# Ten gates projected inside a merge stage: all in the first two branches, or spread over four

## The chip, the cores and the metric

One core of a Trainium2 chip runs the whole program, one decoder layer on 1024 tokens of width 1024. The time is device microseconds of one execution, as the median of several runs; smaller is better. Engines are named as the profile names them: PE is the matmul engine (PEld its weight loads), DVE the vector engine, ACT the scalar engine, POOL GpSimd, and SP the engine whose queue issues every DMA of this kernel.

## The reference, cut to what matters

The mixer projects the normalised input h to the inputs of four token mixers and to four gates of 1024 channels. The outputs of the mixers are projected, multiplied by the sigmoid of their gate, summed, and projected once more.

```python
z = h @ w_in
(u_a, q_b, k_b, v_b, q_c, k_c, v_c, q_d, k_d, v_d, qi_d, ki_d, wi_d, gates) = jnp.split(z, SPLIT_POINTS, axis=-1)
o_a = conformer_conv(...); o_b = diff_attention(...)
o_c = stick_breaking_attention(...); o_d = dsa_attention(...)
g = sigmoid(gates).reshape(b, s_len, 4, 1024)
merged = g[:, :, 0] * (o_a @ w_branch[0])
for i, o in ((1, o_b), (2, o_c), (3, o_d)):
    merged = merged + g[:, :, i] * (o @ w_branch[i])
return merged @ w_out
```

A gated FFN follows, which the change doesn't touch.

## The kernel before

All tiles are held transposed, 128 channels on the partitions and 1024 tokens along the free axis. There are 4 x 8 = 32 gate tiles; (br, c) is channel block c of branch br. Matmuls work on two float32r parts, high and low: split_w (L178) loads a raw weight tile of 512 KB into one of two wr buffers, casts the high part on ACT and subtracts the low part on POOL, or on the engine handed in. A gate projection, proj (L356), takes 2 halves x 8 k x 3 products, 48 matmuls, and reads the input hH and hL; its weights lie in the four wp buffers, a pair for each gate. Its results go through two PSUM buffers (pmm).

The first 22 gates in the order of the list gq (L540) are projected ahead of the merge by gate_tile (L542), which stores the raw result in the scratch sg_s; PE does that between the steps of the attention branches. Ten are left in gq when the merge begins.

The merge (L902) goes through the branches in the order 3, 2, 1, 0. For each it splits two k halves of the branch's output (from o_s) and of its weights (L905, L908, low parts on DVE), eight tiles of the twelve in pool obp; then for each c it gets the gate in a buffer sg, one of three in pool sgp. Where the gate is still in gq it is projected there and ACT writes its sigmoid out of PSUM (L914): a live gate. Otherwise SP loads it from the scratch and ACT applies the sigmoid in place (L917). A branch tile of 12 matmuls (L925) goes into one of two PSUM buffers (pss); DVE multiplies it by sg (L928), and for all but the first branch the product is added to accs[c] (L930), on POOL for branches 2 and 1, on DVE for branch 0. As gq keeps (2,6), (2,7) and (3,0) to (3,7), all live gates lie in the first two branches of the merge.

Behind it the sum is split into mhi (ACT, L947) and mlo (DVE, L948), in two halves of 512 tokens, and the output projection (L968) runs over row tiles t. Half 0 lies in pool big, which is opened where hH and hL end; half 1 in pool mg, which is opened where sgp ends.

The order of instructions on each engine is fixed at build time by a planner: it goes by program order, but puts what it holds to be ready ahead of what it holds to be waiting; buffers of one pool go round in program order. On the chip each engine takes its instructions in that order and waits where one isn't ready.

Of the kernel before, what the change touches and what calls it, by code (L numbers as in the profile page):

```python
# [25 lines left out]
NK = D // P  # L26
# [86 lines left out]
def tile_hybrid_block(ctx, tc, x, pos, ada, pk, cst, w_in, w_br, w_out, w_up, w_dn, out):  # L113
    nc = tc.nc

    def pool(name, bufs, space=None, side=None):
        kw = {} if space is None else {"space": space}
        return tc.tile_pool(name=name, bufs=bufs, side=side, reuse_waits="tile", **kw)
# [3 lines left out]
    def dma(o, i):  # L122
        return nc.sync.dma_start(o, i)  # L123
# [54 lines left out]
    def split_w(src, wpool=None, E=None):  # L178
        wpool = wpool or wp
        raw = wr.tile([P, D], F32, name="wraw", tag="w")  # L180
        dma(raw, src)
        hi = wpool.tile([P, D], F32R, name="whi", tag="w")
        lo = wpool.tile([P, D], F32R, name="wlo", tag="w")
        A.copy(hi, raw)  # L184
        (E or G).tensor_tensor(out=lo, in0=raw, in1=hi.bitcast(F32), op=OP.subtract)  # L185
        return hi, lo
# [72 lines left out]
    pmm = psx.enter_context(pool("pmm", 2, PSUM))  # L259
    ptt = psx.enter_context(pool("ptt", 2, PSUM))  # L260

    NSPILL = 22
    HP = 100000
    hi_pri = ExitStack()
    mrg = ExitStack()
# [3 lines left out]
    with ExitStack() as mix:  # L269
# [86 lines left out]
        def proj(name, i, consume):  # L356
            hi, lo = split_w(w_in[W_INDEX[(name, i)]])
            for hf in range(2):
                ps = pmm.tile([P, 512], F32, name="mm", tag="mm")
                n = 0  # L360
                cs = slice(hf * 512, hf * 512 + 512)
                for k in range(NK):
                    ks = slice(k * P, (k + 1) * P)
                    for a, b in ((hi, hH), (hi, hL), (lo, hH)):
                        PE.matmul(ps, a[:, ks], b[:, k, cs], start=(n == 0), stop=(n == 3 * NK - 1))  # L365
                        n += 1
                consume(hf, cs, ps)
# [121 lines left out]
        with pool("scp", 1) as scp, ExitStack() as scx:  # L489
# [47 lines left out]
                proj(name, i, consume)  # L537
                store_hl(name, i, hi, lo, 2, 64, False)

            gq = [(br, c) for br in range(4) for c in range(NK)]  # L540

            def gate_tile():  # L542
                br, c = gq.pop(0)

                def consume(hf, cs, ps):
                    o = gtp.tile([P, 512], F32, name="gt", tag="g")
                    A.copy(o, ps)
                    dma(sg_s[br * NK + c][:, cs], o)
                proj("g", br * NK + c, consume)
# [35 lines left out]
            with pool("rad", 1) as rad, pool("radj", 1) as radj, pool("rada", 1) as rada:  # L585
# [58 lines left out]
                for t in A_T + V_T:  # L644
                    c = off[t - 2]
# [4 lines left out]
                for t in A_T + V_T:  # L650
# [5 lines left out]
                    c = off[t - 2]  # L656
# [196 lines left out]
                dma(o_s[2 + pr], oT)  # L853

        hi_pri.close()
        while len(gq) > 32 - NSPILL:
            gate_tile()

        hcs = []
# [41 lines left out]
        with pool("sgp", 3, side="right") as sgp:  # L901
            for bi, br in enumerate((3, 2, 1, 0)):  # L902
                oh, ol, wh, wl = [], [], [], []
                for k in range(2):
                    hi, lo = split_w(o_s[2 * br + k], obp, V)  # L905
                    oh.append(hi)
                    ol.append(lo)
                    a, b = split_w(w_br[2 * br + k], obp, V)  # L908
                    wh.append(a)
                    wl.append(b)  # L910
                for c in range(NK):
                    sg = sgp.tile([P, S], F32, name="sgl", tag="w")
                    if (br, c) in gq:
                        proj("g", br * NK + c, lambda hf, cs, ps: A.activation(sg[:, cs], ps, AF.Sigmoid))  # L914
                    else:
                        dma(sg, sg_s[br * NK + c])
                        A.activation(sg, sg, AF.Sigmoid)  # L917
                    ccs = slice(c * P, (c + 1) * P)
                    ps = pss.tile([P, S], F32, name="brp", tag="s")
                    for hf in range(2):  # L920
                        cs = slice(hf * 512, hf * 512 + 512)
                        n = 0
                        for k in range(2):
                            for a, b in ((wh, oh), (wh, ol), (wl, oh)):
                                PE.matmul(ps[:, cs], a[k][:, ccs], b[k][:, cs], start=(n == 0), stop=(n == 5))  # L925
                                n += 1
                    dst = accs[c] if bi == 0 else sg
                    V.tensor_tensor(out=dst, in0=ps, in1=sg, op=OP.mult)  # L928
                    if bi:
                        (G if br else V).tensor_tensor(out=accs[c], in0=accs[c], in1=sg, op=OP.add)  # L930
# [199 lines left out]
def build(nc, arrays):  # L1130
    import concourse.tile as _tile
    args = {n: nc.dram_tensor("in_" + n, a.shape, mybir.dt.from_np(a.dtype), kind="ExternalInput").ap()
            for n, a in arrays.items()}
    o = nc.dram_tensor("out_y", (S, D), F32, kind="ExternalOutput").ap()
    with _tile.TileContext(nc) as tc:  # L1135
        r = tile_hybrid_block(tc, *args.values(), o)
    return r
# [10 lines left out]
```

## Time and profile before

| | us |
|---|---|
| three runs, median | 2032.14 |
| lowest and highest | 2029.38, 2036.47 |
| profiled execution | 2032.69 |
| its span, first to last instruction | 2030.9 |
| PE busy | 1855.4 (91% of the span) |
| DVE busy | 1154.4 (57%) |
| ACT busy | 829.5 (41%) |
| POOL busy | 472.9 (23%) |

The rows below come from one profiled execution. Times of a row are microseconds from the start of the span. A row of the timeline gives start, duration, engine, line, operation, what it writes and reads, its count where several are merged, and in brackets how long the engine had stood idle before it and what ended that. PE rows overlap, as matmuls are pipelined: the distance of two starts, not the duration, is what one costs. A row of the table by stretches gives, for each engine, its busy time and instructions, then the granted clock of PE (1.00 is full speed), the share of DMA time and the GB/s.

### The profile page before, as it was taken

Reading aid. Unit: us, or ns where it says so; the run is one execution under the profiler, and the core shown is the slowest. Engines: PE = TensorE matmul, PEld = TensorE weight load, DVE = VectorE, ACT = ScalarE, POOL = GpSimd, SP = SyncE. Lnnn points to the kernel's source line nnn. Section 1 sums busy time; section 2 is a strip of 40 time slices with the busy share of each in tenths; the row PEclk is TensorE's granted clock in tenths of the full one; section 3 lists DMA queues with packets and bytes.
Section 4 is the critical chain, followed back from the end, with each engine's and each line's share of the span. In section 5 each row is a group of like instructions: output and inputs, shape, how many; then the busy total and the mean of one; then the engine's idle time right before and its main releaser. Section 6 shows DMA issues by size and latency. Waiting matters only on the chain. (4 is left out here: it accounts for less than half of the span.)

```text
span 2030.9 us, 22858 instructions
## 1 busy us (share of the span) xinstructions
PE 1855.4 (91%) x8792; PEld 1443.3 (71%) x8792; DVE 1154.4 (57%) x1731; ACT 829.5 (41%) x1458; POOL 472.9 (23%) x244
## 2 busy tenths in 40 slices
PE   6888877499999999899999899999999999999996
PEld 3655555376767776677787668788888888888875
DVE  6759999605899857685113765532343334433457
ACT  5556666236545645463222444333122212221122
POOL 0102145272111110011205610222122212222024
PEclk9988989699999999899999999999999999999999
DMA  8364423444514242513113632121111101111114
GB/s 312 94 165 151 174 84 93 126 92 104 187 57 125 78 129 69 147 42 115 62 63 129 225 122 83 63 73 42 32 63 58 47 32 52 62 52 42 32 62 145
DMA packets 61038, 197.30 MB, mean 97 GB/s; under 512 B 9153, under 2 KB 9281, under 8 KB 60929
## 3 DMA queue, kind: packets, MB, share of 16 engines
q1 hardware_dynamic: 60928, 195.84, 30.6%
q8 instruction: 69, 1.13, 0.2%
q14 instruction: 41, 0.33, 0.1%
HBM read 154.13 MB, written 41.68 MB: 96 GB/s over the span
## 5 line engine op out<-in xcount | busy, mean ns | idle before, releaser
L185 POOL TENSOR_TENSOR wlo<-wraw,whi 128x1024 fp32r<-128x1024 f32 x126 | 317.4, 2521 | 1384.2 <-ACT whi L184 1348.2
L365 PE MATMUL mm<-hH,whi 128*128 128x512 f32 x864 | 353.5, 409 | 49.6 <-ACT whi L184 31.5
L365 PE MATMUL mm<-hH,wlo 128*128 128x512 f32 x864 | 350.4, 406 | 3.7 <-POOL wlo L185 3.7
L365 PE MATMUL mm<-hL,whi 128*128 128x512 f32 x864 | 351.9, 407 | 0.9 <-DVE hL L321 0.9
L184 ACT CAST whi<-wraw 128x1024 fp32r<-128x1024 f32 x144 | 150.6, 1049 | 413.2 <-PE ups L1017 283.7
L1017 PE MATMUL ups<-h2h,whi 128*128 128x512 f32 x704 | 277.6, 395 | 1.3 <-DVE h2h L994 1.3
L1017 PE MATMUL ups<-h2l,whi 128*128 128x512 f32 x704 | 277.5, 394 | 0.5 <-DVE h2l L995 0.5
L1017 PE MATMUL ups<-h2h,wlo 128*128 128x512 f32 x704 | 274.5, 390 | 0.0
L1022 DVE SCALAR_TENSOR_TENSOR u<-ups,pkt,u 128x1023 f32<-128x1023 f32 x44 | 56.4, 1283 | 350.8 <-ACT u L1021 350.8
L365 PEld LDWEIGHTS mm<-hH,whi 128*128 128x128 f32 x864 | 166.6, 193 | 95.6 <-ACT whi L184 32.0
L365 PEld LDWEIGHTS mm<-hH,wlo 128*128 128x128 f32 x864 | 166.5, 193 | 41.4 <-POOL wlo L185 4.8
L365 PEld LDWEIGHTS mm<-hL,whi 128*128 128x128 f32 x864 | 167.2, 194 | 36.1 <-issue 2.6
L1017 PEld LDWEIGHTS ups<-h2h,whi 128*128 128x128 f32 x704 | 132.6, 188 | 32.3 <-DVE h2h L994 1.7
L1017 PEld LDWEIGHTS ups<-h2h,wlo 128*128 128x128 f32 x704 | 132.5, 188 | 29.8
L1017 PEld LDWEIGHTS ups<-h2l,whi 128*128 128x128 f32 x704 | 132.7, 189 | 28.2 <-DVE h2l L995 1.0
L1052 DVE TENSOR_TENSOR ya<-ya,dps 128x1024 f32<-128x1024 f32 x80 | 97.3, 1217 | 58.8 <-PE dps L1047 58.6
L605 DVE TENSOR_SCALAR_CACHE_REDUCE junkb<-key,cf 128x1024 bf16<-128x1024 uint16 (+3 forms) x124 | 117.3, 946 | 4.3
L1047 PE MATMUL dps<-whi,ah 128*128 128x512 f32 x352 | 109.4, 392 | 5.5 <-DVE ya L1052 5.5
L1047 PE MATMUL dps<-wlo,ah 128*128 128x512 f32 x352 | 108.6, 390 | 0.0
L1047 PE MATMUL dps<-whi,al 128*128 128x512 f32 x352 | 108.4, 389 | 0.0
L872 DVE SCALAR_TENSOR_TENSOR hc<-hpad,pkt,hc 128x1024 f32<-128x1024 f32 x60 | 84.2, 1408 | 0.0
L1047 PEld LDWEIGHTS dps<-whi,ah 128*128 128x128 f32 x352 | 65.4, 188 | 22.2 <-DVE ya L1052 8.9
(560 smaller groups left out, 2950.3 us busy)
## 6 DMA issues: line engine op xcount, KB each, us to landing
wraw<-in_w_in SPq DMA_DIRECT2D x54, 512.0 KB, 3.9
adaw<-in_ada SPq DMA_DIRECT2D x48, 512.0 KB, 5.9
wraw<-in_w_up SPq DMA_DIRECT2D x44, 512.0 KB, 3.3
sg_s<-gt SPq DMA_DIRECT2D x44, 256.0 KB, 2.6
sgl<-sg_s SPq DMA_DIRECT2D x22, 512.0 KB, 3.4
wraw<-in_w_dn SPq DMA_DIRECT2D x22, 512.0 KB, 3.3
xt<-in_x SPq DMA_DIRECT2D x16, 512.0 KB, 4.9
qis<-qk_s SPq DMA_DIRECT2D x16, 256.0 KB, 4.2
```

Of the source, the lines that this page charges most:

```text
L184: A.copy(hi, raw)
L185: (E or G).tensor_tensor(out=lo, in0=raw, in1=hi.bitcast(F32), op=OP.subtract)
L365: PE.matmul(ps, a[:, ks], b[:, k, cs], start=(n == 0), stop=(n == 3 * NK - 1))
L605: V.tensor_scalar(out=j[:, :n], in0=src, scalar1=scal, scalar2=None, op0=op, op1=OP.add, accum_out=dst[:, kc(t):kc(t) + 1])
L872: V.scalar_tensor_tensor(out=hc, in0=hpad[:, k:k + S], scalar=w(k), in1=hc, op0=OP.mult, op1=OP.add)
L1017: PE.matmul(ps[:, hf * 512:hf * 512 + 512], a[:, ks], b, start=(n == 0), stop=(n == 23))
L1022: V.scalar_tensor_tensor(out=u[:, 1:], in0=ps[:, 0:S - 1], scalar=w(1), in1=u[:, 1:], op0=OP.mult, op1=OP.add)
L1047: PE.matmul(ps[:, cs], a[:, tb], b[:, cs], start=(n == 0), stop=(n == tot - 1))
L1052: V.tensor_tensor(out=ya[t], in0=ya[t], in1=ps, op=OP.add)
```

## The change

The list of live gates is written out: (br, 2) and (br, 5) for every branch, and (3,0) and (0,7), again ten. gq holds the other 22, and all of them go through the scratch ahead of the merge; the merge asks for membership in LIVE instead of gq. In the order of the merge branch 3 now has live gates at c = 0, 2, 5, branches 2 and 1 at c = 2, 5, and branch 0 at c = 2, 5, 7.

```diff
-    NSPILL = 22
+    LIVE = {(br, c) for br in range(4) for c in (2, 5)} | {(3, 0), (0, 7)}
...
-            gq = [(br, c) for br in range(4) for c in range(NK)]
+            gq = [(br, c) for br in range(4) for c in range(NK) if (br, c) not in LIVE]
...
-        while len(gq) > 32 - NSPILL:
+        while gq:
             gate_tile()
...
-                    if (br, c) in gq:
+                    if (br, c) in LIVE:
                         proj("g", br * NK + c, lambda hf, cs, ps: A.activation(sg[:, cs], ps, AF.Sigmoid))
```

## Rows read from the trace of the kernel before

**Rows 1.** From the page, PE's busy time in the whole span.

```profile
PE 1855.4 (91%) x8792; PEld 1443.3 (71%) x8792; DVE 1154.4 (57%) x1731; ACT 829.5 (41%) x1458; POOL 472.9 (23%) x244
```

**Rows 2.** Table by stretches: PE, PEld, DVE, ACT, POOL busy, clock, DMA, GB/s.

```profile
970.00:1020.00 50.00, 49.27 (x215) 40.42 (x216) 4.90 (x4) 8.18 (x13) 7.21 (x3) 1.00 0.18 62
...
1115.00:1150.00 35.00, 30.09 (x113) 23.06 (x114) 19.32 (x15) 14.57 (x14) 22.07 (x9) 0.90 0.64 225
1150.00:1178.00 28.00, 24.27 (x99) 18.91 (x98) 27.76 (x23) 14.05 (x17) 14.29 (x5) 0.94 0.56 186
```

**Rows 3.** Timeline of PE: first matmuls of gates, branch tiles and output projection.

```profile
964.00 0.40 PE L925 MATMUL brp<-whi 128*128 128x512 f32 x1
...
970.73 0.50 PE L365 MATMUL mm<-hH,whi 128*128 128x512 f32 x1 [1.07 <-ACT sgl L914]
...
1036.88 0.40 PE L365 MATMUL mm<-hH,whi 128*128 128x512 f32 x1
...
1047.88 0.40 PE L925 MATMUL brp<-whi 128*128 128x512 f32 x1
...
1050.65 0.40 PE L365 MATMUL mm<-hH,whi 128*128 128x512 f32 x1
...
1171.49 0.50 PE L968 MATMUL yps<-whi,mhi 128*128 128x512 f32 x1
```

**Rows 4.** Timeline of PE: the waits in the back of the merge.

```profile
1116.12 0.60 PE L925 MATMUL brp<-whi,wlo 128*128 128x512 f32 x1 [2.33 <-DVE wlo L185]
...
1135.73 0.50 PE L925 MATMUL brp<-whi 128*128 128x512 f32 x1 [0.34 <-DVE sgl L928]
...
1140.55 0.50 PE L925 MATMUL brp<-whi 128*128 128x512 f32 x1 [1.10 <-DVE sgl L928]
...
1143.56 0.71 PE L925 MATMUL brp<-whi 128*128 128x512 f32 x1 [2.05 <-ACT whi L184]
...
1157.86 0.80 PE L925 MATMUL brp<-whi 128*128 128x512 f32 x1 [2.79 <-DVE sgl L928]
...
1168.63 0.50 PE L925 MATMUL brp<-whi 128*128 128x512 f32 x1 [0.94 <-DVE sgl L928]
```

**Rows 5.** Timeline of SP, ACT, POOL and DVE behind the turn 3 to 2.

```profile
1067.08 1.47 SPq L123 DMA_DIRECT2D wraw<-in_w_in  x2
...
1071.66 1.05 ACT L184 CAST whi<-wraw 128x1024 fp32r<-128x1024 f32 x1 [1.18 <-DMA wraw<-in_w_in]
...
1073.81 2.41 POOL L185 TENSOR_TENSOR wlo<-wraw,whi 128x1024 fp32r<-128x1024 f32 x1
...
1071.73 1.22 DVE L928 TENSOR_TENSOR sgl<-brp,sgl 128x1024 f32<-128x1024 f32 x1 [0.36 <-PE brp L925]
```

**Rows 6.** Behind the turn 2 to 1: a stretch, then rows of the timeline.

```profile
1116.10:1119.50 3.40, 3.38 (x8) 2.62 (x9) 0.11 (x1) 0.58 (x1) 0.00 (x0) 0.54 0.87 320
...
1120.19 1.05 ACT L184 CAST whi<-wraw 128x1024 fp32r<-128x1024 f32 x1 [0.21 <-DMA wraw<-o_s]
...
1120.69 11.46 POOL L930 TENSOR_TENSOR macc<-macc,sgl 128x1024 f32<-128x1024 f32 x4 [5.71 <-DVE sgl L928]
...
1121.30 1.22 DVE L928 TENSOR_TENSOR sgl<-brp,sgl 128x1024 f32<-128x1024 f32 x1 [0.68 <-PE brp L925]
```

**Rows 7.** Timeline of POOL and DVE behind the turn 1 to 0.

```profile
1149.87 5.72 POOL L185 TENSOR_TENSOR wlo<-wraw,whi 128x1024 fp32r<-128x1024 f32 x2 [5.89 <-ACT whi L184]
...
1150.44 1.22 DVE L928 TENSOR_TENSOR sgl<-brp,sgl 128x1024 f32<-128x1024 f32 x1
```

**Rows 8.** Timeline of ACT, DVE and PE at the way into the output projection.

```profile
1179.94 4.78 ACT L947 CAST mhi<-macc 128x512 fp32r<-128x512 f32 x9
...
1180.59 7.28 DVE L948 TENSOR_TENSOR mlo<-macc,mhi 128x512 fp32r<-128x512 f32 x9 [2.31 <-ACT mhi L947]
...
1184.25 0.50 PE L968 MATMUL yps<-whi,mhi 128*128 128x512 f32 x1 [2.69 <-ACT mhi L947]
...
1187.32 0.80 PE L968 MATMUL yps<-whi,mlo 128*128 128x512 f32 x1 [1.30 <-DVE mlo L948]
```

## The prediction

> **What bounds the kernel now.** I read the page first: TensorE is busy for 91% of the span [rows 1], so a change of order can only win back time in which PE stands still or runs at the lower clock. Then the busy time of each engine by stretch [rows 2]: at 970 to 1020, where the live gates of branch 3 are projected, PE is busy for 49.27 of 50 us at full clock, with DVE, ACT and POOL nearly empty; at 1115 to 1150 PE has 30.09 of 35 us at a granted clock of 0.90, at 1150 to 1178 24.27 of 28 us at 0.94, with DVE full (27.76 of 28). So the merge stage has a front that PE bounds and a back, fed from the scratch, in which PE waits for others.
>
> Third, PE in order of time, for what the stage would take without waits. A gate projection (48 matmuls) goes from 1036.88 to 1047.88, 11.0 us; a branch tile (12 matmuls) from 1047.88 to 1050.65, 2.77 us [rows 3], or 0.23 us a matmul. The stage runs from the first branch matmul at 964.00 to the first matmul of the output projection at 1171.49 [rows 3]: 207.5 us. Nine gates lie in it (the tenth, (3,0), already runs earlier, under the layer norm of branch 0), so PE needs 9 x 11.0 + 32 x 2.77 = 187.6 us. **19.9 us** is all that this stage can give. The named waits of it are in [rows 4]: 2.33 at 1116.12 (for the split of branch 1), 0.34 at tile (1,7), 1.10 and 2.05 at the turn to branch 0, 2.79 and 0.94 within branch 0; the clock falls after the long ones: 8 matmuls took 3.4 us at 1116.1 to 1119.5 with 0.54 granted [rows 6], 3.4 - 8 x 0.23 = 1.6 us lost.
>
> **What the change moves.** Ten live gates before and after, and 22 through the scratch before and after: the number of projections, stores, loads, sigmoids and splits is equal, and so is everything ahead of the merge (the 22 early gates are the same work with other indices): 0. Only places change: branch 3 has live gates at c = 0, 2, 5, branches 2 and 1 at 2 and 5, branch 0 at 2, 5, 7.
>
> **Gain: the back of the stage is thinned.** In branch 0 DVE multiplies, adds and splits the sum; it is the bound there (27.76 of 28 us [rows 2]), and PE waits for it. With three gates between them PE has 3 x 11.0 + 8 x 2.77 = 55 us of work beside 8 x 2 x 1.22 = 20 us of DVE (1.22 a tile by its row in [rows 5]). The waits 2.79 and 0.94 go, and the half clock that follows the first. The clock 0.94 over 28 us [rows 2] means 12% of it at half speed, 3.4 us, of which half is lost: 1.7 us. The 0.34 at (1,7) comes of a run of 8 scratch tiles through three sg buffers; with (1,5) live the next are loaded ahead. Sum 2.79 + 0.94 + 1.7 + 0.34 = 5.8; the waits of under 0.3 us in the same tiles bring it to about **6.5 us** (bounds 5.8 and 7.5). POOL has per branch 8 adds and 2 splits, about 10 x 2.4 = 24 of 44 us, and ACT less: neither becomes a bound. Branch 3 now reads five gates from the scratch; the first, (3,1), needs a buffer in the memory of hc, which a store still reads, but PE has gate (3,2) to do from 970.73 [rows 3] for 11 us, and needs that tile's PSUM buffer only after it: 0, and a wait of PE at (3,3) if the gate comes after 982. SP carries as many issues as before, in another order.
>
> **Not gained: the turns of the branches.** The second half of a branch's operands (k = 1: four tiles of obp, which has 12) waits for the last matmuls of the branch before. After the change this is still a turn from scratch tile c = 7 to scratch tiles c = 0, 1. The 2.33 and its clock stay: the k = 1 split needs the same obp tiles, and POOL adds beside it as now; at the turn to branch 0 the 2.05 was for an ACT cast [rows 4] that stood behind a sigmoid; with gates loaded earlier I take 1 of it as gained (bounds 0 and 2).
>
> **Loss: the weights of the first live gate of a branch come late.** split_w has two wr buffers, taken in program order; while a branch's k = 1 operands wait in both, no gate's weights can be loaded. The rows show it at the turn 3 to 2: the two next gates are loaded only at 1067.08, the first is cast at 1071.66 and its low part is there at 1073.81 + 2.41 = 1076.2 [rows 5]. Behind such a wait in PE's queue stands the rest of the branch, and DVE and POOL wait with it. It cost nothing before, since six tiles of branch 2 stood ahead of (2,6). Now two stand ahead of (2,2), done at 1071.7, when DVE takes (2,1) [rows 5]. Each such wait has two ends. If PE's fixed order has the gate right behind them, it waits 4.5 us less the two matmuls that need only the high part: 4.0. If tile (2,3) is put ahead, it starts when DVE has freed the PSUM buffer of (2,1), 1073.0, ends at 1075.8 and 0.4 stay: 1.3 + 0.4 = 1.7. At the turn 2 to 1: cast at 1120.19, then one of the four adds of 11.46 us on POOL, 1120.69 to 1123.5, then the split, to 1126.4; PE is free at 1121.2 [rows 6]: 4.7, or 1.3 + 1.1 = 2.4. At the turn 1 to 0, where DVE adds and POOL is free: split 1149.87 + 5.72/2 = 1152.7, PE free at 1150.3 [rows 7]: 1.9, or 1.4. Sum **5.5** with the tile put ahead, **10.6** without, and then the clock falls after the two long ones, 2 x 1.6: 13.8. I take 5.5: the planner that orders PE puts what is ready first (from 964.00 to the next gate matmul at 970.73 [rows 3] it ran two tiles, (3,0) and (3,1), ahead of that gate, whose PSUM was not free), and a tile whose gate is still being loaded is ready. Were POOL to take the split before the add, the 0.4 and 1.1 would go and 4.0 stay; the lower bound is 0, if a gate's load took a wr buffer ahead of the k = 1 operands, which program order speaks against.
>
> **Loss or gain: the way into the output projection.** mhi and mlo of half 0 are in pool big, opened where hH and hL were, and these now are read to the end of gate (0,7). Of the 16 casts of each kind 9 were left at 1179.94 [rows 8], so 7 had been done during branch 0; now these 7 too start only when that gate ends, 2.77 us ahead of the output projection. They are 0.53 us each on ACT and 0.81 on DVE (9 in 4.78 and in 7.28 us [rows 8]); PE takes 3 matmuls for each c in two row tiles, 1.4 us, so it is slower than they. On the other side DVE has no backlog any more, and today's 2.69 and 1.30 [rows 8] can shrink. Bounds -4.0 (both go) and +4 (mlo at double length, from contention with POOL); I take -1.
>
> **Sum** for the likeliest: -6.5 - 1 + 5.5 - 1 = -3.0 us. The profiled execution took 2032.69 us, 1.8 of it outside its span of 2030.9, and lies 0.55 above the median of the three runs: 2029.7 for its like, 2029 as a median.
>
> A row that speaks against the change: after 2.33 us of idle the matmuls ran at a granted clock of 0.54 [rows 6]. [...]
>
> **Rivals.** (a) *Late weights in program order, slower.* PE's order is (c 0, c 1, gate 2) and each of the three gates is waited for: 10.6 us, and all three restarts at the low clock, 3 x 1.6 = 4.8, against 6.5 gained and nothing at the turns or the end: +8.9, **2041**. It decides from 12.6 us of waits on (6.5 + 6.1). For it: PE's queue is fixed at build time, and the 2.33 shows that the planner does not foresee POOL in DVE's way. Against it: tile (3,1) ahead of its gate. (b) *The waits are covered, faster.* POOL takes the splits ahead of the adds, 4.0 us remain, the ACT wait of the turn goes whole, and so do the 2.69 and 1.30 at the end: -6.5 - 2 + 4.0 - 4.0 = -8.5, **2023.5**. For it: every one of these is a matter of order alone; against it: three orders must all fall well. (c) *The end pays.* As forecast but with +4 at the way into the output projection: +2, 2034, still no change. (d) *Nothing moves*: were the planner to pull the live gates together again, all would stay at 2032; against it, the gates pass through three sg buffers in program order.
>
> **How the numbers follow.** About 0.3% (6.1 us) is what a measurement of this kernel can tell from no change. Forecast and (c), (d): 0.50 together, all within 0.3%; (b) 0.27; (a) 0.23. The range takes in (b) and most of what it would be with no wait for weights at all (-12.5), so from -11, 2021; and (a) to just past its price, 2042.
>
> **What would show it.** Right: in the profile after, PE in branch 0 without waits for DVE and at full clock from its second tile; the same wait for the DVE split at the turns 2 to 1; loads of in_w_in issued just behind each turn; PE waits for whi or wlo ahead of the first live gate of branches 2, 1, 0, about 1 to 3 us each; mhi casts all after gate (0,7). Wrong: the raw weights of (2,2) loaded before the turn (then no such waits), or long waits of PE at the entry into the output projection (over 4 us more than today's 4.0), or a stage ahead of 964 that has moved.

## The result, and the profile after

The changed kernel takes **2044.51 us** (median of 5 runs, 2042.42 to 2047.37) against 2035.17 us (5 runs, 2029.38 to 2038.16) for the kernel before: a ratio of 1.0053, 95% interval 1.0034 to 1.0071. It is slower by about half a per cent; forecast were 2029 us and no measurable change. The profiled execution took 2042.42 us with a span of 2040.6 us, 9.7 us longer than the span of before.

PE's busy time (the page, first part) rose from 1855.4 us [rows 1] by 14.5 us, with the same 8792 matmuls: the work is the same, so part of it ran at a lower clock.

```profile
PE 1869.9 (92%) x8792; PEld 1452.7 (71%) x8792; DVE 1150.5 (56%) x1731; ACT 830.9 (41%) x1458; POOL 470.3 (23%) x244
```

Where it happened is seen in a table by stretches of the kernel after (columns as in [rows 2]): the last row is branch 0, where PE, at 24 to 30 busy of 28 to 35 us before, now has 46.70 of 46.70 us at full clock, as forecast. But the four stretches above it, which hold matmuls and nearly no idle time, have a granted clock of 0.68 to 0.87.

```profile
972.70:986.60 13.90, 13.88 (x48) 11.23 (x49) 2.45 (x2) 4.12 (x5) 0.00 (x0) 0.78 0.42 155
1025.70:1037.70 12.00, 11.92 (x45) 9.54 (x46) 2.63 (x2) 2.60 (x3) 4.69 (x3) 0.86 0.64 216
1078.20:1089.80 11.60, 11.54 (x45) 9.39 (x46) 2.62 (x2) 2.60 (x3) 4.68 (x3) 0.87 0.58 198
1122.20:1127.40 5.20, 5.13 (x16) 4.02 (x17) 1.65 (x3) 2.11 (x2) 3.12 (x2) 0.68 0.36 112
1130.00:1176.70 46.70, 46.70 (x205) 38.22 (x204) 15.34 (x14) 12.52 (x17) 11.35 (x5) 1.00 0.25 86
```

What stands ahead of each of those four is seen in the timeline of PE after. It begins with the first gate behind the layer norm (the row of before is 970.73 [rows 3]); then come the first live gates of branches 2 and 1, the turn 1 to 0, the first gate of branch 0 and the start of the output projection:

```profile
972.72 0.80 PE L365 MATMUL mm<-hH,whi 128*128 128x512 f32 x1 [2.92 <-ACT sgl L914]
...
1025.78 0.50 PE L365 MATMUL mm<-hH,wlo 128*128 128x512 f32 x1 [2.72 <-POOL wlo L185]
...
1078.26 0.79 PE L365 MATMUL mm<-hH,wlo 128*128 128x512 f32 x1 [2.64 <-POOL wlo L185]
...
1120.10 0.50 PE L925 MATMUL brp<-whi 128*128 128x512 f32 x1 [1.30 <-ACT whi L184]
...
1122.27 0.79 PE L925 MATMUL brp<-whi,wlo 128*128 128x512 f32 x1 [0.97 <-DVE wlo L185]
...
1127.35 0.40 PE L365 MATMUL mm<-hH,whi 128*128 128x512 f32 x1
...
1176.78 0.40 PE L968 MATMUL yps<-whi,mhi 128*128 128x512 f32 x1
```

The merge runs from its first branch tile at 964.17 (964.00 before [rows 3]) to 1176.78, 212.6 us for the 207.5 of before. Counting each gate at 11.0 us and each branch tile at 2.77 us, as the prediction does, both need 187.6 us; what is left over, stretch by stretch, from the starts in PE's timeline:

| lost in the merge, us | before | after |
|---|---|---|
| start, to the turn 3 to 2 | 1.3 | 5.8 |
| turn 3 to 2 | 1.5 | 1.4 |
| gate (2,2): wait and clock | 0 | 4.7 |
| turn 2 to 1 | 5.6 | 3.8 |
| gate (1,2): wait and clock | 0 | 4.3 |
| turn 1 to 0 and branch 0 | 11.4 | 5.2 |
| small rest | 0.1 | -0.2 |
| sum | 19.9 | 25.0 |

To the +5.1 of the merge comes +4.4 behind it: from the start of the output projection to the end of the span it is 2030.9 - 1171.49 = 859.4 us before and 2040.6 - 1176.78 = 863.8 us after. With 0.2 ahead of the merge that is the 9.7. So there are three losses: **the start** (4.5), **the late weights** (9.0) and **the tail** (4.4); and one gain, 1.8 + 6.2 = 8.0 at the later turns and in branch 0.

### The profile page after: what moved, and what is told of

Same layout as the page of the kernel before. It is cut to its first block, busy times and chain, and to the rows that moved or that the text cites. A ratio compares the mean times of both kernels' runs of the same rounds, so it can differ in the third digit from the quotient of the medians.

```text
span 2040.6 us, 22854 instructions
## 1 busy us (share of the span) xinstructions
PE 1869.9 (92%) x8792; PEld 1452.7 (71%) x8792; DVE 1150.5 (56%) x1731; ACT 830.9 (41%) x1458; POOL 470.3 (23%) x244
## 5 line engine op out<-in xcount | busy, mean ns | idle before, releaser
L365 PE MATMUL mm<-hH,whi 128*128 128x512 f32 x864 | 358.8, 415 | 45.8 <-ACT whi L184 25.4
L365 PE MATMUL mm<-hL,whi 128*128 128x512 f32 x864 | 356.1, 412 | 1.2 <-DVE hL L321 1.2
```

## Experiments

All are timed against the kernel before; e1 to e5 ran together (before 2034.64 us there), e6 to e9 together (2033.68) and e10 and e11 together (2034.07). "Merge" is its length in the profiled execution, "behind" the span from the start of the output projection on.

| run | us | ratio, 95% interval | merge | behind |
|---|---|---|---|---|
| the change | 2044.51 | 1.0053, 1.0034 to 1.0071 | 212.6 | 863.8 |
| e1_own_raw | 2029.28 | 0.9973, 0.9960 to 0.9987 | 200.2 | 863.2 |
| e2_pool_split | 2039.89 | 1.0026, 1.0015 to 1.0038 | 206.1 | 864.0 |
| e4_t7 | 2047.43 | 1.0057, 1.0038 to 1.0075 | 209.0 | 867.1 |
| e5_all | 2029.80 | 0.9975, 0.9960 to 0.9990 | 192.9 | 866.5 |
| e6_last | 2039.87 | 1.0030, 1.0017 to 1.0044 | 209.4 | 863.5 |
| e7_all_last | 2025.71 | 0.9962, 0.9946 to 0.9977 | 193.0 | 863.2 |
| e8_c47 | 2045.72 | 1.0059, 1.0044 to 1.0074 | 214.7 | 863.4 |
| e9_all_sg4 | 2024.93 | 0.9956, 0.9942 to 0.9970 | 193.2 | 863.1 |
| e10_tail | 2036.43 | 1.0017, 1.0007 to 1.0028 | 209.4 | 858.4 |
| e11_all_tail | 2021.29 | 0.9939, 0.9927 to 0.9951 | 193.1 | 857.1 |

The merge of e4_t7, e6_last and e10_tail is untouched by their edits and still took 209.0 to 209.4 us, not 212.6: how much clock was granted behind the same waits differs from one execution to the next (last section). Medians and intervals decide; the merge length tells where.

### The late weights (theory W)

The rows of the profile after that show the mechanism, on SP, ACT and POOL behind the turn 3 to 2:

```profile
1016.60 1.47 SPq L123 DMA_DIRECT2D wraw<-in_w_in  x2
...
1020.02 1.06 ACT L184 CAST whi<-wraw 128x1024 fp32r<-128x1024 f32 x1 [2.80 <-DMA wraw<-in_w_in]
...
1021.03 2.40 POOL L930 TENSOR_TENSOR macc<-macc,sgl 128x1024 f32<-128x1024 f32 x1 [52.70 <-DVE sgl L928]
1023.38 2.35 POOL L185 TENSOR_TENSOR wlo<-wraw,whi 128x1024 fp32r<-128x1024 f32 x1
```

The weights of (2,2) are loaded only when the branch's own operands have left the two wr buffers. In POOL's order an add stands ahead of the split: POOL, idle for 52.70 us, takes up the add at 1021.03, and the cast that the split needs ends at 1021.08; so wlo is there only at 1025.73, and PE begins at 1025.78. Both things make this wait. An estimate from the rows: had the split come first, at 1021.08, wlo would have been there 2.35 us later, at 1023.43, and PE, which stood idle from 1023.06, would have waited 0.4 us instead of 2.72. At the turn 2 to 1, where the cast ends at 1072.70 and POOL has an add from 1073.51 and the split from 1075.86, it would not have waited at all. A kernel with POOL's order alone changed wasn't run. PE's fixed order was a third one, neither of the two that the prediction priced: four matmuls of the gate that need only the high part, three matmuls of tile (2,3), then the wait. For the test the live gates of branches 2, 1 and 0 get raw buffers of their own, so that their loads depend on no operand of the branch:

```diff
-        with pool("sgp", 3, side="right") as sgp:
+        with pool("sgp", 3, side="right") as sgp, pool("wgp", 2, side="right") as wgp:
...
-                        proj("g", br * NK + c, lambda hf, cs, ps: A.activation(sg[:, cs], ps, AF.Sigmoid))
+                        proj("g", br * NK + c, lambda hf, cs, ps: A.activation(sg[:, cs], ps, AF.Sigmoid),
+                             wgp if br < 3 else None)
...
-        raw = wr.tile([P, D], F32, name="wraw", tag="w")
+        raw = (rpool or wr).tile([P, D], F32, name="wraw", tag="w")
```

> The changed kernel, but the raw weights of the live gates of branches 2, 1 and 0 get two buffers of their own, so that they no longer stand behind the k = 1 operands. Nothing else is changed. Theory W (the weights of a branch's first live gate come too late): PE's waits for the low part at 1025.78 (2.72 us) and 1078.26 (2.64 us) go, and with them the half clock behind them (the 44 matmuls after each took 11.9 and 11.5 us for 10.1): 8.5 us; besides, the gate's matmuls now can fill the waits at the three turns (about 0.8, 3.0 and 3.0 us and a half clock of 1.6): 2044.5 becomes 2028 to 2036. Rival E (the loss lies at the two ends of the merge, ahead of 972 and in the output projection): at most 2 us change.

Measured: 2029.28 us, the merge 12.4 us shorter than that of the change. The waits of PE within the merge of e1_own_raw (summed by what ended them: us, times, longest; its L926 is L925 of the change):

```profile
PE brp L926 <- ACT whi L184: 4.5, 3, 3.0
PE mm L365 <- ACT sgl L914: 2.9, 1, 2.9
PE brp L926 <- DVE wlo L185: 0.4, 1, 0.4
```

and the same of the change:

```profile
PE mm L365 <- POOL wlo L185: 5.4, 2, 2.7
PE mm L365 <- ACT sgl L914: 2.9, 1, 2.9
PE brp L925 <- ACT whi L184: 2.6, 2, 1.3
PE brp L925 <- DVE wlo L185: 2.2, 3, 1.0
PE brp L925 <- DVE sgl L928: 1.4, 2, 0.7
```

No wait for POOL's wlo is left, and none for DVE's products (sgl L928): with the weights at hand, PE does gate matmuls while the turn's operands are split. W holds, as far as the weights' coming late is the cause; the run doesn't tell the wait for a buffer from POOL's order, as weights that come early are also split ahead of the adds. The gain is larger than the two waits and their clock (9.0) because the turn 1 to 0 shrinks too, from 5.2 to about 2 us; the turn 2 to 1, where PE still waits 2.99 us, doesn't. What stays is the wait at the start (2.9) and the one for the cast of the next branch's operands.

The opposite test moves the live gates instead: to c = 4 and 7, far behind the turns, with the wr buffers as they are.

```diff
-    LIVE = {(br, c) for br in range(4) for c in (2, 5)} | {(3, 0), (0, 7)}
+    LIVE = {(br, c) for br in range(4) for c in (4, 7)} | {(3, 0), (3, 2)}
```

> The changed kernel with its own two raw buffers and only the places of the live gates changed: c = 4 and 7 of every branch, with (3,0) and (3,2); again ten, and 22 through the scratch. Theory W (what costs is that only two tiles stand between a turn and the first live gate, while its weights take some 11.8 us from the turn): four tiles, 11.1 us, stand there now, so PE's waits for the low part of a gate's weights (2.7 and 2.6 us) and the half clock behind them go: -8.5 us; the start of the merge may come right as well (-4.7), as the raws of two more gates of branch 3 keep branch 2's operands out of the layer norm: 2031 to 2036. Rival (it is the sharing of the buffers as such, or spreading the gates at all): the waits stay, 2042 to 2046.

Measured: 2045.72 us, no better than the change. The waits for POOL's wlo fell from 5.4 to 0.3 us, as W says; but others came in their place, at the start and for the products (waits of PE within the merge of e8_c47):

```profile
PE brp L925 <- DVE sgl L928: 6.0, 4, 3.6
PE mm L365 <- ACT sgl L914: 5.9, 1, 5.9
PE brp L925 <- DVE wlo L185: 4.8, 3, 2.3
...
PE mm L365 <- POOL wlo L185: 0.3, 1, 0.3
```

So these other places alone do not help. At the start the rows show why: ACT stands idle for 3.78 us for an operand loaded from o_s and casts it at 973.85, ahead of the sigmoid that frees PE's buffer (976.21). What makes the products late there wasn't tried.

### The start (theory S)

Ahead of the first gate matmul of the merge, DVE ends the layer norm (L891, two multiplies), ACT applies it and then writes the sigmoid that frees the gate's PSUM buffer (L914). The rows of before (DVE, ACT):

```profile
963.73 2.36 DVE L891 TENSOR_TENSOR hc<-hc,rst 128x1024 f32<-128x1024 f32 x2
...
970.08 1.09 ACT L914 ACTIVATE sgl<-mm 128x512 f32<-128x512 f32 x2
```

and after (DVE, POOL, ACT):

```profile
963.79 1.16 DVE L185 TENSOR_TENSOR wlo<-wraw,whi 128x1024 fp32r<-128x1024 f32 x1
964.87 4.55 DVE L891 TENSOR_TENSOR hc<-hc,rst 128x1024 f32<-128x1024 f32 x2
...
965.32 3.01 POOL L185 TENSOR_TENSOR wlo<-wraw,whi 128x1024 fp32r<-128x1024 f32 x1 [15.64 <-ACT whi L184]
...
972.07 1.09 ACT L914 ACTIVATE sgl<-mm 128x512 f32<-128x512 f32 x2
```

Branch 3 has three live gates now instead of eight, so the raw buffers pass to branch 2's first operands while the layer norm still runs, and their split (DVE, 1.16 us) stands ahead of L891. L891 itself, begun 1.14 us later, then takes 4.55 us for its two multiplies instead of 2.36, beside a POOL split that begins 0.45 us behind its own start. (Before, POOL's split began at 965.15, in the second multiply, and it was POOL that took longer, 3.21 us.) The sigmoid comes 2.0 us later, PE waits 2.92 us instead of 1.07, and the 48 matmuls behind the wait take 13.91 us (972.72 to 986.63) for 11.0.

The Trainium skill, SBUF — State Buffer, section SBUF: two separate sides, says that DVE and GpSimd share one port pair as an exclusive lock: the instruction that starts first holds it to its end and the other is blocked, where DVE reads two inputs from SBUF and GpSimd reads SBUF too. The trace agrees: POOL's split comes between the two multiplies and ends at 968.33, and one more multiply of 1.18 us from there (half of the 2.36 of before) gives 969.5, where the two multiplies end (964.87 + 4.55 = 969.42).

The test puts the two early splits on POOL, so that DVE goes from its reciprocal straight to the two multiplies:

```diff
-                    hi, lo = split_w(o_s[2 * br + k], obp, V)
+                    E = G if br == 2 and k == 0 else V
+                    hi, lo = split_w(o_s[2 * br + k], obp, E)
...
-                    a, b = split_w(w_br[2 * br + k], obp, V)
+                    a, b = split_w(w_br[2 * br + k], obp, E)
```

> The changed kernel, but the low parts of branch 2's first operands (k = 0) are subtracted on POOL and not on DVE; in the changed kernel these two run on DVE between the steps of the layer norm of branch 0. Theory S (the start): the first sigmoid of the merge comes at 970 again and not at 972, PE's wait ahead of its first gate falls from 2.92 to about 1.1 us and the 48 matmuls behind it run at full clock, 11.0 for 13.9 us: -4.7 us, 2040. Rival (the start is set by the layer norm's own steps, or POOL's subtractions block DVE as much): within 1 us of 2044.5.

Measured: 2039.89 us, 4.6 below the change; the two multiplies back at 2.36 us, PE's wait at 1.09 us, and the 48 matmuls behind it in 11.1 us (timeline of e2_pool_split, DVE and PE):

```profile
967.76 2.36 DVE L891 TENSOR_TENSOR hc<-hc,rst 128x1024 f32<-128x1024 f32 x2
...
974.77 0.51 PE L365 MATMUL mm<-hH,whi 128*128 128x512 f32 x1 [1.09 <-ACT sgl L915]
...
1025.06 0.50 PE L365 MATMUL mm<-hH,wlo 128*128 128x512 f32 x1 [2.69 <-POOL wlo L185]
```

S holds, and it is independent of W: the wait of 2.69 for the late weights is still there. The edit takes away two things at once, the split ahead of L891 and the collision; neither was taken away alone. An estimate from ACT's rows after: its first step of the layer norm (L892) ends at 968.70, and the second begins at 969.51, behind L891; so the collision cost about 0.8 of the 2.0 us by which the sigmoid came later, and the split ahead the rest.

### The tail (theories E and Q)

At the end of the output projection PE's order has the transposes of row tile 6 (h2t) ahead of the last matmul of tile 7 (timeline of PE after):

```profile
1282.48 1.87 PE L989 MATMUL h2t<-ctile,xt 128*128 128x128 f32 x8 [2.50 <-DVE xt L981]
1284.00 0.78 PE L968 MATMUL yps<-whi,mlo 128*128 128x512 f32 x1
...
1297.03 1.04 PE L989 MATMUL h2t<-ctile,xt 128*128 128x128 f32 x8
...
1301.43 0.73 PE L1017 MATMUL ups<-h2h,whi 128*128 128x512 f32 x2 [3.36 <-DVE h2h L994]
```

Theory E was that this one matmul, late by the wait of 2.50, makes the tail late. First all matmuls of tile 7 were put ahead in the planner's order:

```diff
+                pri = ExitStack()
+                if t == NT - 1:
+                    pri.enter_context(tc.high_priority(HP))
                 for hf in range(2):
...
+                pri.close()
```

> The changed kernel, but the matmuls of the last row tile (t = 7) of the output projection have priority with the planner, so that its last matmul no longer stands behind the transposes of row tile 6 in PE's queue. Theory E (order at the end of the output projection): the last matmul of the projection comes some 4 us earlier, and with it the chain to the FFN: -4 to -5 us, 2040. Rival (the chain of DVE and ACT steps of tiles 6 and 7 sets the start of the FFN, whichever matmul is last): within 1 us of 2044.5.

Measured: 2047.43 us and 867.1 us behind the merge: the tail is 3.3 us longer, not shorter, while the interval of the time overlaps that of the change. The projection's last matmul came earlier, but PE then stood still for 3.94 us elsewhere:

```profile
1279.66 0.77 PE L1021 MATMUL ups<-h2h,whi 128*128 128x512 f32 x1 [3.94 <-DVE jk L979]
```

The same with the two other edits in it:

> All three at once: own raw buffers for the live gates, branch 2's first low parts on POOL, priority for the last row tile. If the three causes add up (theories W, S and E): -17 to -26 us against the changed kernel, 2018 to 2027, which is 5 to 16 us faster than the kernel before. If they cover one another, no faster than the best of the three alone.

Measured: 2029.80 us; the merge is down to 192.9 us, so the gains of W and S add up, and the tail of 866.5 us is that of e4_t7. Then the priority was kept for the last three matmuls alone:

```diff
+                            with ExitStack() as pri:
+                                if t == NT - 1 and hf and k == NK - 1:
+                                    pri.enter_context(tc.high_priority(HP))
+                                PE.matmul(ps[:, hf * 512:hf * 512 + 512], a[half][:, k, tl], b,
...
```

> The changed kernel, but only the last three matmuls of the last row tile of the output projection have priority; the order is that of the changed kernel, except that the one matmul that stood behind the transposes of row tile 6 now stands ahead of them. Theory E2 (that one matmul is what holds up row tile 7): it runs at about 1280 and not at 1284, the chain behind it ends 3.5 to 4 us earlier: 2040.5. Rival (at the end the DVE and ACT steps of row tiles 6 and 7 are the bound, as the run with priority for the whole tile suggests): at most 1 us.

> Own raw buffers for the live gates, branch 2's first low parts on POOL, and the last three matmuls of the output projection first. By the sum of the parts (merge start to end of the span: own buffers -13.0 by the trace, POOL split -4.7, last matmul -4 by theory E2 or 0): 2023 or 2027. Rival: the parts cover one another, no better than own raw buffers alone (2029.3).

Measured: in e6_last the last matmul starts at 1278.78, ahead of h2t, and yet 863.5 us behind the merge, no gain. E falls: tile 7's transposes start 15.7 us after the end of its last matmul there (1279.18 to 1294.92), 11.7 us before (1275.64 to 1287.32). (The median of e6_last, 2039.87, lies 4.6 below that of the change; its tail doesn't explain that, its merge of 209.4 may; the two intervals overlap.) e7_all_last, with W's and S's edits, is at 2025.71 us, faster than the kernel before.

A side question was whether the waits that stay at the turns, for ACT's cast of the next operands, come from the three sg buffers (theory G). e9_all_sg4 is e7_all_last with four:

```diff
-        with pool("sgp", 3, side="right") as sgp, pool("wgp", 2, side="right") as wgp:
+        with pool("sgp", 4, side="right") as sgp, pool("wgp", 2, side="right") as wgp:
```

> As the run with own raw buffers, POOL split and last matmuls first, but with four sg buffers and not three. At the turns 2 to 1 and 1 to 0 PE still waits 1.2 to 3.0 us for ACT's cast of k = 1 operands, which stands behind a sigmoid that waits for a gate's load. Theory G (the load is late because three buffers are too few across a turn): with a fourth the waits fall under 0.5 us: -2 to -4 against three buffers. Rival (the cast waits for the obp buffers, not for the sigmoid): no change.

Measured: 2024.93 us, not to be told from e7_all_last, with the same waits (1.23 and 1.12 us for whi, 1.52 and 1.20 there). G falls.

What keeps tile 7 is seen on ACT. Before, the square of tile 7 and its square root (L250) run ahead of the eight evictions of tile 6's transposes (L991):

```profile
1277.48 1.00 ACT L973 ACTIVATE jk<-yps 128x1024 f32<-128x1024 f32 x1
...
1278.80 0.20 ACT L250 ACTIVATE sm<-sm 128x1 f32<-128x1 f32 x1 [0.22 <-DVE sm L249]
1280.37 2.90 ACT L991 ACTIVATE jk<-h2t,B,A 128x128 f32<-128x128 f32 x8 [1.37 <-PE h2t L989]
```

After, square and root both stand behind them:

```profile
1283.87 2.92 ACT L991 ACTIVATE jk<-h2t,B,A 128x128 f32<-128x128 f32 x8 [3.44 <-PE h2t L989]
1286.64 1.07 ACT L973 ACTIVATE jk<-yps 128x1024 f32<-128x1024 f32 x1
...
1288.88 0.20 ACT L250 ACTIVATE sm<-sm 128x1 f32<-128x1 f32 x1 [1.08 <-DVE sm L249]
```

In e6_last the square has moved ahead, the root of 0.2 us has not: it is at 1284.99, behind the evictions of 1282.24. Theory Q: this root holds up tile 7. The test puts ahead the chain of tile 7, from its square to the sum xt, together with the last three matmuls:

```diff
+                pri = ExitStack()
+                if t == NT - 1:
+                    pri.enter_context(tc.high_priority(HP))
                 A.activation(jk, ps, AF.Square, accum_out=sm[:, 0:1])
                 rstd_of(sm[:, 0:1], sm)
...
                 V.tensor_tensor(out=xt, in0=xt, in1=jk, op=OP.add)
+                pri.close()
```

> The changed kernel with two things put ahead in the planner's order: the last three matmuls of the output projection, as in e6_last, and the chain of tile 7 from its square (L973) to the sum xt (L976). Theory Q: in the profile after and in that of e6_last ScalarE's square root of tile 7 (L250, 0.20 us, in program order behind the eight evictions h2t of tile 6 at L991, 2.9 us) holds up the whole chain of tile 7: 15.7 us from the last matmul to tile 7's transposes in e6_last, 11.7 before. In this kernel the root stands behind one eviction, not eight, so that theory Q expects 11.5 to 13 us there, span minus start of the output projection 859.4 to 860.8 (863.5 to 863.8 without) and a median 3 to 4 us below that of e6_last, so 2036 to 2037. Rival: the end is set by something else (the FFN's first loads, or tile 6's own chain); then span minus start stays at 863 to 864 and the median at 2039 to 2045.

> e10_tail's edit together with the gates' own raw buffers (e1_own_raw) and the splits of the first operands of branch 2 on GpSimd (e2_pool_split). Theory Q: merge 193 us as in e7_all_last, span minus start of the output projection 859.4 to 860.8 in place of 863.2, median 3 to 4 us below e7_all_last: about 2022. Rival: no gain over e7_all_last, 2025 to 2026.

Measured: e10_tail 2036.43 us with 858.4 us behind the merge, e11_all_tail 2021.29 us with 857.1. ACT in e10_tail (the edits move L991 to L998):

```profile
1280.39 0.46 ACT L998 ACTIVATE jk<-h2t,B,A 128x128 f32<-128x128 f32 x1 [1.87 <-PE h2t L996]
1280.75 0.19 ACT L250 ACTIVATE sm<-sm 128x1 f32<-128x1 f32 x1
1280.84 2.54 ACT L998 ACTIVATE jk<-h2t,B,A 128x128 f32<-128x128 f32 x7
```

The root now stands behind one eviction, and the transposes of tile 7 come 13.0 us after the end of the last matmul (1277.34 to 1290.34), for 11.5 to 13 expected; the span behind the merge is shorter even than the 859.4 of before, 5.1 us less than in e6_last. Counted from the start of the projection the transposes come 2.7 us earlier than there (116.4 for 119.1), and behind them PE waits for h2h 0.58 us instead of 3.34. Each of the six runs of e11_all_tail is below each of the six of e7_all_last, and eleven of the twelve of e10_tail below all of e6_last. Q holds in this form: the order of tile 7's chain is what held the tail up. The edit puts the whole chain ahead; that the root is the step that counts is read from the rows, as no run moved it alone. With all three edits the merge takes 193.1 us, 5.5 above what PE needs, and the kernel is 0.6% faster than the one before (0.9939, 0.9927 to 0.9951). How much of that is due to the spread gates isn't shown: the same edits weren't made to the kernel before. In it PE's waits within the merge are down to

```profile
PE brp L927 <- ACT whi L184: 3.1, 3, 1.3
PE mm L365 <- ACT sgl L915: 1.1, 1, 1.1
PE brp L927 <- DVE wlo L185: 0.5, 2, 0.2
```

Why the planner orders tile 7's chain otherwise after the change is open: nothing in that part of the program was edited, and every variant with another place of the gates or other buffers kept a tail of 863 to 864 us until the order was forced.

## Why the prediction was wrong, step by step

**What bounds the kernel: right.** The back of the merge, fed from the scratch, was where PE waited, and thinning it pays: branch 0 now runs without a wait behind its turn.

**The gain: right in kind, its size in part by luck.** Forecast were 6.5 for branch 0 and 1 at the turn 1 to 0; that stretch gave 6.2 (11.4 to 5.2). The turn 2 to 1 was to stay; it gave another 1.8, and together they make 8.0 for 7.5. But the waits of that turn did stay: 0.73 and 2.33 before, 0.71, 1.27 and 1.02 after. What is gone is the low clock behind them, and in e4_t7, with 0.71, 1.48 and 0.80 at the same place, it is there again (last section). So these 1.8 aren't shown to be the change's.

**The late weights: foreseen, but their price too low.** The sum took 1.7 + 2.4 + 1.4 = 5.5 for waits and left the clock to the slower rival, at 1.6 for each restart. Measured are two waits of 2.72 and 2.64 us, 5.4 in all, and none in branch 0, where DVE adds and POOL is free to split: the sum of the waits came out by luck, as none of its three terms did. And the 44 matmuls behind them took 11.91 us (1025.78 to 1037.69) and 11.53 us (1078.26 to 1089.79) for 10.1: 1.8 and 1.4 us more for the clock. With small remainders that is 9.0 for 5.5. (As the last section shows, the 1.8 came up in this execution and in none of four others with the same wait.) The step that failed is the choice to price waits of 1.4 to 2.4 us at nothing but their length, when the row beside it (2.33 us of idle, then 0.54 granted [rows 6]) showed what follows one of that length. The order of PE was neither of the two ends either; planned orders come in more kinds than "ahead" and "behind".

**Ahead of the merge and the start of branch 3: the 0 was wrong by 4.5.** The step that failed is the 0 for everything ahead of the merge, and with it the start of gate (3,2) taken over from before, 970.73. The number of instructions is the same; but fewer live gates in branch 3 hand the raw buffers on sooner, and what comes next through them, branch 2's operands, is split by DVE in the middle of a chain on which PE waits. The prediction followed the wr buffers at every turn but not at this first one. e2_pool_split shows the loss and gives it back.

**The way into the output projection: the entry right, the end missed.** At the entry PE waits 0.76 and 1.96 us for mlo and 1.62 us for the diagonal of the row that is spread there, for 2.69 and 1.30 before [rows 8]: 4.3 for 4.0. But there the granted clock fell in the kernel before, and it doesn't in the kernel after (a stretch of each in this order, columns as in [rows 2]):

```profile
1171.40:1202.70 31.30, 27.31 (x103) 20.42 (x102) 19.51 (x32) 13.48 (x21) 5.85 (x2) 0.89 0.29 101
1176.70:1207.00 30.30, 25.81 (x103) 18.11 (x101) 23.15 (x35) 14.89 (x24) 10.72 (x3) 1.00 0.35 130
```

So the first 96 of the projection's 384 matmuls take 30.2 us after for 31.2 before: the -1 that was forecast, but by the clock and not by shorter waits. The loss, 5.4, arises at the last two row tiles, 105 us later, which no step of the prediction looked at; with the -1.0 that is the +4.4. Rival (c) had +4 at this place, by contention at the entry; the size came out, the mechanism didn't.

**The sum.** -8.0 of gain, +9.0 of late weights, +4.5 at the start, +4.4 in the tail and -0.2 of small items in the merge and ahead of it make +9.7. Against the forecast of -3.0, some 3.5 came from the late weights, 4.5 from the start and 5.4 from the end of the output projection. The slower rival (a) gave 2041 by the late weights in program order and their clock; the time came out 3.5 above it, with half of its waits (5.4 for 10.6), with about its price for a restart (1.8 and 1.4 for 1.6) at two of its three places, and with two causes that it didn't have.

## What to carry to other kernels

When work is moved to another place in a rotation of buffers, follow the buffers to their next user at every place where the count changed, and ask what that user's first instruction pushes back on its own engine. Give the weights that must arrive at a turn buffers of their own: here two tiles turned a loss of 0.5% into a gain of 0.3%. Where a planner fixes the order, an untouched stage can come out in another order; look at the last tiles of a stage, where the order of one tile's chain, with a root of 0.2 us behind eight evictions, cost about 5 us (863.5 for 858.4).

## What the runs showed of the hardware

Waits of PE of 2.6 to 2.9 us cost up to as much again in clock, but not each time. Behind the start wait, 2.86 to 2.92 us in all of these, 48 matmuls took 13.9 us in the change (972.72 to 986.63), 13.9 in e1_own_raw (972.63 to 986.55) and 12.5 in e10_tail (973.05 to 985.59), for 11.0 at full clock; behind the wait for (2,2), 2.70 to 2.72 us, 44 took 11.9 in the change and 10.2 in e10_tail, for 10.1. A row of e10_tail for that last stretch reads 1.00, where the change has 0.86:

```profile
1024.80:1035.00 10.20, 10.20 (x45) 8.39 (x46) 1.47 (x2) 2.29 (x3) 4.68 (x2) 1.00 0.57 185
```

Five profiled executions have these waits: the change, e2_pool_split, e4_t7, e6_last and e10_tail. Behind (2,2) the clock is low in the change alone (44 matmuls in 10.2 us in the four others). Behind (1,2), after 2.64 or 2.65 us of waiting, they took 11.5 to 11.6 us in four; in e4_t7, after 2.13 us, 10.2.

Shorter waits close together were followed by it too. Behind those of the turn 1 to 0 (in the change 0.71, 1.30 and 0.97 us) the next 15 matmuls took 5.1 us for 3.5 in all five. Behind nearly the same three waits of the turn 2 to 1 they took 3.6 us in four, and 5.1 us only in e4_t7:

```profile
1065.80:1071.00 5.20, 5.16 (x16) 4.12 (x17) 1.23 (x1) 2.20 (x3) 0.86 (x1) 0.67 0.32 106
```

A single wait of about 1.1 us at the start left the matmuls behind it at full clock in e2_pool_split and e11_all_tail (48 in 11.1 us). What decides which execution is granted the clock isn't shown.

Two multiplies of DVE took 4.55 us instead of 2.36 when a POOL split (3.01 us) began in the first of them, and 2.36 when it began in the second; then POOL took 3.21 us. POOL began 0.45 us behind the start of the first multiply in the one case (after) and 1.42 us behind it in the other (before).
